# A two-layer hybrid decoder trunk on one core: residual rows, layer parameters and weight buffers placed differently

## The chip, the core and the metric

One core of a Trainium2 chip runs the whole program. TensorE (PE) does the matrix products, VectorE (DVE), ScalarE (ACT) and GpSimd (POOL) the elementwise work, and SyncE (SP) issues every DMA. The metric is the device time of one execution in microseconds, lower is better.

## What is computed

x is 1024 tokens by 1024 features in float32. Two layers (DEPTH = 2), each of them:

```
h = RMSNorm(x);  z = h @ w_in                       (1024 x 2560)
u = c_a * sigmoid(c_g);  u = silu(LayerNorm(dwconv31(u)))        (512 channels)
o = (softmax(q1 k1) - lam * softmax(q2 k2)) v      (4 heads, causal, rotary)
lam = exp(sum(lq1*lk1)) - exp(sum(lq2*lk2)) + lam_init
o = RMSNorm(o) * subln_g * (1 - lam_init)
x = x + RMSNorm(concat(u, o) @ w_out)
f = RMSNorm(x) @ w_up;  f = dwconv3(f);  f = gelu(f_g) * f_v
x = x + RMSNorm(f @ w_down)
```

The first four lines and w_out are called the mix here, the last two lines of the layer the FFN (up and down).

## The kernel before

Every float32 product runs as three passes (hi by hi, lo by hi, hi by lo). A weight block is therefore split: ACT copies the raw block to its rounded part (`whw`, `whq`, `wo`, `wp`; L460 and L1280), then DVE or POOL subtracts to get the rest (`wlw`, `wlq` at L466; L1281). A 512-wide product of one 128x128 block is one matmul; `hA` and `hB` hold the normalised rows of tokens 0 to 511 and 512 to 1023, transposed, in both parts.

A layer's mix (from L415) is ordered by a planner, `Flow` (L103): generators book time on four clocks (PE, DVE, ACT, POOL), wait for named events (`fl.set`), and take slots of rings (`Ring`) that stand for the tile buffers; a table of PE work (`TOKS`), one of conv taps (`TAPS`) and one of heads (`SEQ`) are its input. What the planner emits is the order of each engine. At the mix's end `wout` (L1059) multiplies by w_out, half of the columns and half of the tokens at a time (`dh`, `b`). `wout_half` (L1115) keeps the first half of the columns of a token tile, and for the second half of the tokens it also takes a buffer of the ring `e` and loads the residual rows x[4 + tt] into it (`xe`). `wout_post` (L1143) does the rest of a tile: the gain (L1154), the square sum on ACT (L1157), the reciprocal root (L350 on DVE, L352 on POOL), residual add (two operations, L1167 and L1168), store, square sum (L1173), root, and the next norm's rows `xn` (L1180). Tiles 0 to 3 take their `xn` from the ring `e` as well.

The FFN's up products run over a written sequence `seq` (L1583), with tasks hung beside its slots; rows of tiles 4 to 7 are transposed in it at L1331, and the products read `px`, `py`, `pz` banks that ACT and DVE empty (L1436 and after). Weight operands go through a ring `wo` of 7 tiles in the pool `fw_`, made by `parts` (L1277).

The down products are seven runs over 11 chunks each, in the order 1, 2, 5, 3, 6, 7, 4 (`run`, L1612), each with four token-tile banks `pd`; a chunk's operands are prepared three chunks ahead (L1280, L1281). During run 7 and run 4 one step of each generator `post_steps(tt)` (L1641) is taken per chunk: it finishes token tiles 0 to 3 (square L1648, gain L1649, root, residual add L1655 and L1656, store L1657, and for layer 0 the next layer's norm L1661 and L1665, transposes L1672, parts L1673 and L1675). Its residual rows come by `load_x` into the ring `xr`, which has two tiles. `end7` (L1714) folds run 7's bank of a tile into `vv`; run 4 then writes the same banks. After run 4, `postnorm` and `prenorm` (L380 to L402, L360 to L370) finish tiles 4 to 7; the next layer's mix begins with the products `pg` and `pa` (L496).

`params(l)` (L270) loads and works out a layer's small tensors; it is called at the start of each mix. PE, DVE, ACT and POOL keep the written order inside these blocks (`manual_schedule`); between the blocks a list scheduler places instructions. An engine executes in order, so an instruction that waits holds what stands behind it on its engine.

## Time and profile before

| | before |
|---|---|
| median of 3 runs | 2342.78 us (2337.95 to 2342.99) |
| profiled execution: time, span | 2336.54 us, 2334.4 us |
| granted TensorE clock, mean | 0.974 |
| PE busy | 2205.1 us, 94% |
| DVE / ACT / POOL busy | 1863.9 / 1126.9 / 829.9 us |

PE is busy for 94% of the span, so about 129 us of it are left in which PE does nothing. The stages of layer 0, by the last or first instruction of a kind: mix to 497.8 us, FFN up to about 945, down to 1176.3; layer 1's mix from 1185.7 to 1663.6, its FFN to the end. In the rows below a wait is the idle time of an engine before an instruction, with the instruction on another engine that ended it.

### The profile page before, as it was taken

How to read it: one execution, taken by the hardware profiler on the slowest of the kernel's cores; microseconds unless marked ns; L12 is line 12 of the kernel's file. 1: busy time of each engine (PE TensorE's matmuls, PEld its weight loads, DVE VectorE, ACT ScalarE, POOL GpSimd, SP SyncE). 2: the span in 40 equal slices, each digit the busy share in tenths (PEclk: the TensorE clock that was granted, in tenths of full speed). 3: DMA queues.
4: the chain of work that ended last, by engine and by line, in shares of the span. 5: the costliest groups of instructions: out<-in, count | busy, mean ns of one | idle time of the engine just before them, and what ended most of it. 6: DMA issues, size and time to landing. Idle time of an engine off the chain costs nothing. (4 is left out here: it accounts for less than half of the span.)

```text
span 2334.4 us, 31508 instructions
## 1 busy us (share of the span) xinstructions
PE 2205.1 (94%) x10568; PEld 1841.9 (79%) x10568; DVE 1863.9 (80%) x3287; ACT 1126.9 (48%) x2458; POOL 829.9 (36%) x894
## 2 busy tenths in 40 slices
PE   6999997989999999999879999979899999999998
PEld 5898895878877878788668988958788778787886
DVE  5988989657888888777669899896578888887777
ACT  4445456545444444544434454565454544445443
POOL 3324312235444544202433143122454555442024
PEclk9999997999999999999989999979999999999999
DMA  4313323544333334933333133235433333348343
GB/s 151 82 51 91 86 68 118 196 173 136 117 121 131 107 134 141 325 102 95 117 102 87 45 91 87 72 116 193 168 134 122 120 124 121 119 145 305 104 144 118
DMA packets 140129, 295.39 MB, mean 127 GB/s; under 512 B 16832, under 2 KB 33984, under 8 KB 139456
## 3 DMA queue, kind: packets, MB, share of 16 engines
q1 hardware_dynamic: 139968, 293.39, 39.3%
q8 instruction: 83, 1.36, 0.2%
q14 instruction: 78, 0.64, 0.1%
HBM read 198.44 MB, written 78.12 MB: 118 GB/s over the span
## 5 line engine op out<-in xcount | busy, mean ns | idle before, releaser
L1634 PE MATMUL pd<-wp,wo 128*128 128x512 f32 x1776 | 410.6, 393 | 10.8 <-DVE vv L1715 8.0
L1634 PEld LDWEIGHTS pd<-wp,wo 128*128 128x128 f32 x1776 | 334.7, 189 | 83.4 <-issue 7.4
L1583 PE MATMUL py<-t,wo 128*128 128x512 f32 x1584 | 377.4, 391 | 4.7 <-DVE cg L1451 4.7
L1583 PEld LDWEIGHTS py<-t,wo 128*128 128x128 f32 x1584 | 296.7, 188 | 73.5 <-ACT wo L1280 8.0
L1281 POOL TENSOR_TENSOR wo<-ws,wo 128x512 fp32r<-128x512 f32 x176 | 252.4, 1446 | 282.7 <-ACT wo L1280 250.9
L1583 PE MATMUL px<-hA,wo 128*128 128x512 f32 x1056 | 261.7, 400 | 14.9 <-ACT ea L1436 14.9
L1583 PEld LDWEIGHTS px<-hA,wo 128*128 128x128 f32 x1056 | 200.6, 191 | 64.0 <-ACT ea L1436 15.4
L1281 POOL TENSOR_TENSOR wo<-raw,wo 128x512 fp32r<-128x512 f32 x132 | 179.3, 1362 | 154.1 <-ACT wo L1280 149.4
L1281 POOL TENSOR_TENSOR wo<-fa,wo 128x512 fp32r<-128x512 f32 x66 | 101.6, 1555 | 322.7 <-ACT wo L1280 300.3
L1280 ACT ACTIVATE wo<-ws 128x512 fp32r<-128x512 f32 x176 | 108.4, 626 | 135.4 <-PE py L1583 49.6
L1469 DVE SCALAR_TENSOR_TENSOR acc<-cg,fw,acc 128x512 f32<-128x512 f32 x176 | 132.6, 753 | 41.7 <-ACT acc L1457 38.1
L594 DVE SCALAR_TENSOR_TENSOR scr<-u,cw,scr 128x256 f32<-128x256 f32 (+2 forms) x288 | 155.7, 558 | 2.0 <-ACT scr L588 1.8
L849 ACT ACTIVATE e<-S,mxv 128x512 f32<-128x512 f32 (+2 forms) x192 | 110.2, 581 | 66.5 <-DVE mxv L844 40.7
L854 POOL TENSOR_TENSOR sm<-sm 128x1 f32<-128x1 f32 x64 | 25.4, 398 | 328.7 <-ACT e L849 325.9
L1457 ACT ACTIVATE acc<-cg,fb,fw 128x512 f32<-128x512 f32 x88 | 68.2, 775 | 148.1 <-DVE cg L1451 148.1
L496 PE MATMUL pq<-whq,hA 128*128 128x384 f32 x512 | 134.8, 344 | 3.6 <-ACT whq L460 3.6
L496 PE MATMUL pq<-whq,hB 128*128 128x384 f32 x512 | 134.2, 343 | 0.0
L1583 PE MATMUL pz<-b,wo 128*128 128x512 f32 x528 | 131.0, 396 | 2.0 <-DVE cv L1451 2.0
L1583 PE MATMUL pz<-t,wo 128*128 128x512 f32 x528 | 130.5, 396 | 0.0
L1583 PEld LDWEIGHTS pz<-b,wo 128*128 128x128 f32 x528 | 98.3, 188 | 28.2 <-issue 5.1
L840 DVE TENSOR_REDUCE mxv<-S 128x1 f32<-128x512 f32 (+2 forms) x192 | 100.4, 547 | 22.9 <-PE S L824 18.2
L1583 PEld LDWEIGHTS pz<-t,wo 128*128 128x128 f32 x528 | 99.0, 188 | 23.6
(279 smaller groups left out, 5012.7 us busy)
## 6 DMA issues: line engine op xcount, KB each, us to landing
raw<-in_wupd SPq DMA_DIRECT2D x104, 512.0 KB, 3.6
fa<-f SPq DMA_DIRECT2D x154, 256.0 KB, 2.7
f<-fs SPq DMA_DIRECT2D x88, 256.0 KB, 3.1
raw<-in_wmix SPq DMA_DIRECT2D x80, 256.0 KB, 3.0
f<-gg SPq DMA_DIRECT2D x66, 256.0 KB, 2.0
raw<-in_wmix SPq DMA_DIRECT2D x64, 192.0 KB, 2.4
qs<-sth SPq DMA_DIRECT2D x64, 128.0 KB, 2.4
os<-onT SPq DMA_DIRECT2D x16, 512.0 KB, 3.0
```

What stands on the lines that cost most here:

```text
L496: mm = pe.matmul(dst, a, b, start=first and k + j == 0, stop=final and k == n - 1 and j == 2)
L594: ve.scalar_tensor_tensor(dst, src, wk, dst, op0=ALU.mult, op1=ALU.add)
L840: ve.tensor_reduce(mv_[:, j:j + 1], S, axis=AX.X, op=ALU.max, negate=True)
L849: se.activation(e[:, c0:c0 + w], S, AF.Exp, bias=mv_[:, 0:1], accum_out=sm[:, j:j + 1])
L854: po.tensor_tensor(sm[:, 0:1], sm[:, 0:1], sm[:, 1:2], op=ALU.add)
L1280: se.activation(w[:, 0], raw, AF.Copy)
L1281: eng.tensor_tensor(w[:, 1], raw, f32(w[:, 0]), op=ALU.subtract)
L1457: se.activation(acc[n, v, hf], C[n][v][:, 2 + hf * HB:2 + hf * HB + HB], AF.Identity, bias=fb[:, mt:mt + 1], scale=fw[:, mt, 2:3])
L1469: ve.scalar_tensor_tensor(dst, c[:, j + hf * HB:j + hf * HB + HB], fw[:, mt, j:j + 1], a, op0=ALU.mult, op1=ALU.add)
L1583: pe.matmul(ps, x, y, start=first and k + j == 0, stop=k == 3 and j == 2, skip_group_check=not first)
L1634: pe.matmul(ps[tt], x, y, start=first and k + n == 0, stop=k == K2 - 1 and n == 2, skip_group_check=not first)
```

## The change

Four edits. (1) `params` is a generator: DMAs first, then the operations, with two buffers per tensor; layer 1's run inside the mix of layer 0 (`next_params`, booked at 200 and 220 us of the planner's clock). (2) The `w` weights of the mix take their two tiles from a pool that lives for the whole program (`w4`, 4 tiles), and 4 of the 7 `wo` tiles of the FFN are the same four. (3) The residual rows of tiles 4 to 7 are loaded only once the four `xn` of tiles 0 to 3 have their buffers (`rows`). (4) The residual rows of `post_steps` go to two dead weight tiles, are loaded ahead of run 7 and refilled after a tile's store; the norm's `xr` tile is taken only then, one more step lies between the store and the square, and `end7` does its four additions first and the four `first_half` (gain and square) after them. No operation of the computation is left out or added.

```diff
@@ -268,37 +268,34 @@
         ve.memset(negh, -0.5)
         def params(l):
-            p = {}
+
             li = 0.8 - 0.6 * math.exp(-0.3 * l)
             def ptile(key, shape):
-                return par.tile(shape, F32, tag=key, name=f"{key}{l}", bufs=1)
-
-            cw = ptile("cw", [P, 4, CK])
+                return par.tile(shape, F32, tag=key, name=f"{key}{l}", bufs=2)
+
+            cw, cv, sg = ptile("cw", [P, 4, CK]), ptile("cv", [P, 3, 4]), ptile("sg", [P, 1])
             sy.dma_start(cw, ap["cw"][l])
+            sy.dma_start(cv, ap["cvec"][l])
+            sy.dma_start(sg, ap["subg"][l])
+            lv = par.tile([P, 4, HD], F32, tag="lv", name="lv", bufs=1)
+            sy.dma_start(lv, ap["lamv"][l:l + 1].broadcast_to([P, 4, HD]))
+            cws, hv, ls, nl = ptile("cws", [P, 4, (CK + 1) // 2]), ptile("hv", [P, 2, 4]), ptile("ls", [P, 2]), ptile("nl", [P, 1])
+            pars[l] = dict(cw=cw, cws=cws, cv=cv, hv=hv, sg=sg, nl=nl)
+            yield
...
             se.activation(ls, ls, AF.Exp)
-            nl = ptile("nl", [P, 1])
             ve.tensor_tensor(nl, ls[:, 1:2], ls[:, 0:1], op=ALU.subtract)
             ve.tensor_scalar(nl, nl, -li, None, op0=ALU.add)
-            p.update(cw=cw, cws=cws, cv=cv, hv=hv, sg=sg, nl=nl)
-            return p
+
+        pars = {}
         x1 = [[dr.tile([P, D], F32, tag=f"x1_{l}_{t}", name=f"x1_{l}_{t}") for t in range(8)] for l in range(DEPTH)]
         x2 = [[dr.tile([P, D], F32, tag=f"x2_{l}_{t}", name=f"x2_{l}_{t}") for t in range(8)] for l in range(DEPTH)]
@@ -424,7 +421,10 @@
                 if l == 0:
                     for t in range(8):
                         late[t] = prenorm(ptr, x0[t] if t < 3 else first_x(t), g_pre, hh[t // 4], t % 4)
-                p = params(l)
+                if l == 0:
+                    for _ in params(0):
+                        pass
+                p = pars[l]
                 wm = ap["wmix"][l]
                 bst = mx.tile([P, 480], F32, tag="bst", name="bst")[:, 0:192].rearrange("p (a b c) -> p a b c", a=8, b=4)
@@ -445,8 +445,11 @@
                     wi = yield from R[tag].get()
                     size, bufs = (768, 4) if tag == "q" else (1024, 2)
-                    hi = mw.tile([P, size], F32R, tag=f"wh{tag}", name=f"wh{tag}", bufs=bufs)
-                    lo = mw.tile([P, size], F32R, tag=f"wl{tag}", name=f"wl{tag}", bufs=bufs)
+                    if tag == "w":
+                        hi, lo = (rw.tile([P, 1024], F32R, tag="w4", name=f"w{part}w", bufs=4) for part in "hl")
+                    else:
+                        hi = mw.tile([P, size], F32R, tag=f"wh{tag}", name=f"wh{tag}", bufs=bufs)
+                        lo = mw.tile([P, size], F32R, tag=f"wl{tag}", name=f"wl{tag}", bufs=bufs)
                     W[key] = hi, lo, wi
                     step = n if n <= HB else n // 2
                     for j in range(n // step):
@@ -1054,7 +1057,7 @@
                     fl.set("oh", h, b)
                     yield fl.now
-                m0s, xe = {}, {}
+                m0s, xe, rows = {}, {}, []
                 def wout(dh, b):
@@ -1134,6 +1137,8 @@
                     fl.set("m0", b, tt)
                     yield t
                     if b == 1:
+                        if ("rows",) not in fl.seen:
+                            yield ("rows",)
                         i = yield from R["e"].get()
                         x = me.tile([P, D], F32, tag="e", name="xe", bufs=E_BUFS)
                         sy.dma_start(x, xres[4 + tt])
@@ -1211,6 +1216,9 @@
                     yield ("hA2",)
                     i = yield from R["e"].get()
                     xn = me.tile([P, D], F32, tag="e", name="xn", bufs=E_BUFS)
+                    rows.append(tt)
+                    if len(rows) == 4:
+                        fl.set("rows")
                     ss = xs.tile([P, 1], F32, tag="ss", name="ss", bufs=3)
                     se.activation(xn, y, AF.Square, accum_out=ss)
                     t = fl.op("act", ac(D) + 0.1)
@@ -1259,6 +1267,16 @@
                 for b in range(2):
                     fl.spawn(conv_ln(b))
                     fl.spawn(load_o(b))
+                def next_params():
+                    g = params(l + 1)
+                    yield 200.0
+                    next(g)
+                    yield 220.0
+                    next(g, None)
+                    fl.op("dve", 1.6)
+
+                if l + 1 < DEPTH:
+                    fl.spawn(next_params())
                 with tc.manual_schedule(engines={mybir.EngineType.PE, mybir.EngineType.DVE,
                                                  mybir.EngineType.Activation, mybir.EngineType.Pool}):
                     fl.run()
@@ -1276,10 +1294,18 @@
                 def parts(raw, eng, pool_=None, tag="wo", bufs=WO_BUFS):
-                    w = (pool_ or fw_).tile([P, 2, HB], F32R, tag=tag, name=tag, bufs=bufs)
+                    if pool_:
+                        w = pool_.tile([P, 2, HB], F32R, tag=tag, name=tag, bufs=bufs)
+                    else:
+                        w = ((rw.tile([P, 1024], F32R, tag="w4", name="wo", bufs=4) if turn[0] % WO_BUFS < 4 else
+                              fw_.tile([P, 1024], F32R, tag=tag, name=tag, bufs=WO_BUFS - 4))
+                             .rearrange("p (a b) -> p a b", a=2))
+                        turn[0] += 1
                     se.activation(w[:, 0], raw, AF.Copy)
                     eng.tensor_tensor(w[:, 1], raw, f32(w[:, 0]), op=ALU.subtract)
                     return w[:, 0], w[:, 1]
+
+                turn = [0]
                 def small(name):
                     return fw_.tile([P, HB], F32, tag="sr", name=name, bufs=4)
@@ -1644,7 +1670,7 @@
                         m0, s2 = m0s[tt]
                         ps1 = u2[tt]
                         y = xs.tile([P, YW], F32, tag="y", name="y", bufs=2)[:, 0:D]
-                        xr = load_x(x1[l][tt])
+                        xr = rows[tt % 2]
                         se.activation(y[:, 0:HB], ps1, AF.Square, accum_out=s2[:, 1:2])
                         ve.tensor_tensor(y[:, HB:D], ps1, g_pf[:, HB:D], op=ALU.mult)
                         yield 1
@@ -1655,8 +1681,12 @@
                         ve.scalar_tensor_tensor(y[:, 0:HB], m0, r, xr[:, 0:HB], op0=ALU.mult, op1=ALU.add)
                         ve.scalar_tensor_tensor(y[:, HB:D], y[:, HB:D], r, xr[:, HB:D], op0=ALU.mult, op1=ALU.add)
                         sy.dma_start(out[tt * P:(tt + 1) * P, :] if last else x2[l][tt], y)
+                        yield 1
+                        if tt < 2:
+                            sy.dma_start(rows[tt % 2], x1[l][tt + 2])
                         if last:
                             return
+                        xr = xs.tile([P, D], F32, tag="xr", name="xn", bufs=XR)
                         ss = xs.tile([P, 1], F32, tag="ss", name="ss", bufs=3)
                         se.activation(xr, y, AF.Square, accum_out=ss)
                         yield 1
@@ -1713,7 +1743,9 @@
                     def end7(tt):
                         ve.tensor_tensor(vv[tt], pa[tt], vv[tt], op=ALU.add)
-                        m0s[tt] = first_half(vv[tt], g_pf[:, HB:D], "m0d")
+                        if tt == 3:
+                            for t in range(4):
+                                m0s[t] = first_half(vv[t], g_pf[:, HB:D], "m0d")
                     def end4(tt):
                         t = 4 + tt
@@ -1737,6 +1769,9 @@
                     else:
                         g_pre = gvec(l + 1, 0)
                         nhA = alloc_h("hA")
+                    rows = [inB[1][:, i:i + 2].rearrange("p a b -> p (a b)") for i in (3, 5)]
+                    for tt in range(2):
+                        sy.dma_start(rows[tt], x1[l][tt])
                     bg = [post_steps(tt) for tt in range(4)]
                     run(7, pa, False, DTAIL, end7)
```

DVE at the border from the mix to the FFN (layer 0; layer 1 has the same). `pw` is a bank of the last w_out products, `xe` the residual rows, `xn` the next norm's rows. Before:

```order
L1167 SCALAR_TENSOR_TENSOR xe_5513<-m0_5469,rs_5651,xe_5513 128x512
L1168 SCALAR_TENSOR_TENSOR xe_5513<-xn_5634,rs_5651,xe_5513 128x512
L350 TENSOR_SCALAR ss_5656<-ss_5656 128x1
L350 TENSOR_SCALAR ss_5664<-ss_5664 128x1
L1180 SCALAR_TENSOR_TENSOR xn_5611<-xe_5350,rs_5662,gb0_2_5249 128x1024
L350 TENSOR_SCALAR ss_5669<-ss_5669 128x1
L1180 SCALAR_TENSOR_TENSOR xn_5620<-xe_5425,rs_5667,gb0_2_5249 128x1024
L1180 SCALAR_TENSOR_TENSOR xn_5634<-xe_5513,rs_5673,gb0_2_5249 128x1024
L1154 TENSOR_TENSOR xn_5679<-pw_5515,gb0_1_4233 128x512
L1162 TENSOR_TENSOR ss_5682<-s2_5520 128x1
L350 TENSOR_SCALAR ss_5682<-ss_5682 128x1
L1167 SCALAR_TENSOR_TENSOR xe_5677<-m0_5519,rs_5685,xe_5677 128x512
```

After:

```order
L1172 SCALAR_TENSOR_TENSOR xe_5535<-m0_5491,rs_5677,xe_5535 128x512
L1173 SCALAR_TENSOR_TENSOR xe_5535<-xn_5658,rs_5677,xe_5535 128x512
L347 TENSOR_SCALAR ss_5688<-ss_5688 128x1
L1172 SCALAR_TENSOR_TENSOR xe_5570<-m0_5541,rs_5686,xe_5570 128x512
L1173 SCALAR_TENSOR_TENSOR xe_5570<-xn_5668,rs_5686,xe_5570 128x512
L347 TENSOR_SCALAR ss_5696<-ss_5696 128x1
L1185 SCALAR_TENSOR_TENSOR xn_5635<-xe_5389,rs_5694,gb0_2_5271 128x1024
L347 TENSOR_SCALAR ss_5704<-ss_5704 128x1
L1185 SCALAR_TENSOR_TENSOR xn_5644<-xe_5447,rs_5702,gb0_2_5271 128x1024
L347 TENSOR_SCALAR ss_5710<-ss_5710 128x1
L1185 SCALAR_TENSOR_TENSOR xn_5658<-xe_5535,rs_5708,gb0_2_5271 128x1024
L1185 SCALAR_TENSOR_TENSOR xn_5668<-xe_5570,rs_5714,gb0_2_5271 128x1024
```

The fourth tile's gain (L1154 on `xn_5679`) stood behind three of the 1024-wide operations L1180; now all four tiles' residual adds (L1172, L1173) stand ahead of the four wide ones (L1185).

DVE at the end of run 7 in layer 0: `y` are the rows of tile 2, `vv` and `m0d` belong to end7. Before:

```order
L1675 TENSOR_TENSOR hA_0_10717<-pt_10979,hA_0_10717 128x4x128
L1665 SCALAR_TENSOR_TENSOR xr_10891<-y_10890,rs_10986,gb1_0_10715 128x1024
L1655 SCALAR_TENSOR_TENSOR y_10954<-m0d_9995,rs_10991,xr_10955 128x512
L1656 SCALAR_TENSOR_TENSOR y_10954<-y_10954,rs_10991,xr_10955 128x512
L1715 TENSOR_TENSOR vv_9482<-pd_10476,vv_9482 128x512
L380 TENSOR_TENSOR m0d_11039<-vv_9482,gb0_3_9426 128x512
L1715 TENSOR_TENSOR vv_9483<-pd_10477,vv_9483 128x512
L380 TENSOR_TENSOR m0d_11044<-vv_9483,gb0_3_9426 128x512
L1715 TENSOR_TENSOR vv_9484<-pd_10478,vv_9484 128x512
L380 TENSOR_TENSOR m0d_11049<-vv_9484,gb0_3_9426 128x512
L1715 TENSOR_TENSOR vv_9485<-pd_10479,vv_9485 128x512
L380 TENSOR_TENSOR m0d_11054<-vv_9485,gb0_3_9426 128x512
```

After:

```order
L1681 SCALAR_TENSOR_TENSOR y_10973<-m0d_10017,rs_11003,wbB_9483 128x512
L1682 SCALAR_TENSOR_TENSOR y_10973<-y_10973,rs_11003,wbB_9483 128x512
L1745 TENSOR_TENSOR vv_9504<-pd_10498,vv_9504 128x512
L1745 TENSOR_TENSOR vv_9505<-pd_10499,vv_9505 128x512
L1745 TENSOR_TENSOR vv_9506<-pd_10500,vv_9506 128x512
L1745 TENSOR_TENSOR vv_9507<-pd_10501,vv_9507 128x512
L377 TENSOR_TENSOR m0d_11053<-vv_9504,gb0_3_9448 128x512
L377 TENSOR_TENSOR m0d_11057<-vv_9505,gb0_3_9448 128x512
L377 TENSOR_TENSOR m0d_11061<-vv_9506,gb0_3_9448 128x512
L377 TENSOR_TENSOR m0d_11065<-vv_9507,gb0_3_9448 128x512
L1305 TENSOR_TENSOR wp_11074<-wb_9488,wp_11074 128x512
```

The wide norm operation of the tile before (L1665) stood ahead of the residual add and of `vv`; it now stands behind end7 (L1695), and the four `vv` follow one another.

ACT at the border from the FFN of layer 0 to the mix of layer 1: `y`, `xr` belong to the norms of tiles 4 to 7, `whw` to the first two weight tiles of the mix. Before:

```order
L360 ACTIVATE xr_11263,ss_11273<-y_11260 128x1024
L392 ACTIVATE y_11303,s2_11045<-s1_9492 128x512
L392 ACTIVATE y_11346,s2_11050<-s1_9493 128x512
L360 ACTIVATE xr_11306,ss_11316<-y_11303 128x1024
L296 ACT_TABLE_LOAD
L296 ACTIVATE ls1_11448<-ls1_11448 128x2
L392 ACTIVATE y_11389,s2_11055<-s1_9494 128x512
L460 ACTIVATE whw_11462<-raw_11464 128x512
L460 ACTIVATE whw_11462<-raw_11466 128x512
L460 ACTIVATE whw_11468<-raw_11470 128x512
L460 ACTIVATE whw_11468<-raw_11472 128x512
```

After:

```order
L463 ACTIVATE whw_11462<-raw_11464 128x512
L463 ACTIVATE whw_11462<-raw_11466 128x512
L1304 ACTIVATE wp_11254<-wb_9495 128x512
L389 ACTIVATE y_11282,s2_11054<-s1_9513 128x512
L357 ACTIVATE xr_11285,ss_11295<-y_11282 128x1024
L389 ACTIVATE y_11325,s2_11058<-s1_9514 128x512
L463 ACTIVATE whw_11468<-raw_11470 128x512
L463 ACTIVATE whw_11468<-raw_11472 128x512
L389 ACTIVATE y_11368,s2_11062<-s1_9515 128x512
L357 ACTIVATE xr_11328,ss_11338<-y_11325 128x1024
```

The four `whw` copies stood behind the last of the norms' squares and behind the table load and Exp of `params`; two of them now stand ahead of the first square (L389), two behind the second, and table load and Exp are gone from here (the load stands ahead of the first softmax Exp of layer 1's mix).

## Rows read from the trace of the kernel before

**Rows 1.** The longest waits of PE over the span: who waited, for which releaser, us in total, times, longest.

```profile
PE px L1583 <- ACT ea L1436: 14.9, 2, 7.4
...
PE pt L367 <- DVE ss L350: 13.4, 1, 13.4
...
PE o L924 <- ACT o L948: 10.4, 6, 2.5
...
PE pg L496 <- ACT whw L460: 9.4, 1, 9.4
...
PE pd L1634 <- DVE vv L1715: 8.0, 4, 7.1
```

**Rows 2.** PE's timeline at the border from mix to FFN, layer 0 and (last row) layer 1: start us, us, operation, count, idle before.

```profile
492.11 0.39 PE L496 MATMUL pw<-wlw,cat 128*128 128x512 f32 x1
...
497.79 5.75 PE L1583 MATMUL px<-hA,wo 128*128 128x512 f32 x24
...
504.05 1.07 PE L1331 MATMUL pt<-ident,xn 128*128 128x128 f32 x8 [0.51 <-DVE ss L350]
...
512.55 11.18 PE L1583 MATMUL px<-hA,wo 128*128 128x512 f32 x36 [7.44 <-ACT ea L1436]
...
1678.36 10.34 PE L1583 MATMUL px<-hA,wo 128*128 128x512 f32 x36 [7.44 <-ACT ea L1436]
```

**Rows 3.** DVE's timeline there, layer 0.

```profile
496.62 0.69 DVE L1154 TENSOR_TENSOR xn<-pw,gb 128x512 f32<-128x512 f32 x1 [0.41 <-PE pw L496]
...
505.59 1.28 DVE L1180 SCALAR_TENSOR_TENSOR xn<-xe,rs,gb 128x1024 f32<-128x1024 f32 x1 [0.44 <-POOL rs L352]
...
506.80 0.68 DVE L1154 TENSOR_TENSOR xn<-pw,gb 128x512 f32<-128x512 f32 x1
...
509.36 0.75 DVE L1167 SCALAR_TENSOR_TENSOR xe<-m,rs,xe 128x512 f32<-128x512 f32 x1 [0.72 <-POOL rs L352]
```

**Rows 4.** ACT's timeline there.

```profile
511.93 0.58 ACT L1436 ACTIVATE ea<-px 128x512 f32<-128x512 f32 x1
```

**Rows 5.** POOL's timeline there.

```profile
484.95 7.53 POOL L1281 TENSOR_TENSOR wo<-raw,wo 128x512 fp32r<-128x512 f32 x6 [0.63 <-ACT wo L1280]
...
496.35 0.54 POOL L352 TENSOR_TENSOR rs<-ss,negh 128x1 f32<-128x1 f32 x1 [3.86 <-DVE ss L350]
```

**Rows 6.** PE's timeline around the end of run 7, layer 0.

```profile
1124.92 5.74 PE L1634 MATMUL pd<-wp,wo 128*128 128x512 f32 x24
...
1137.71 5.37 PE L1634 MATMUL pd<-wp,wo 128*128 128x512 f32 x12 [7.05 <-DVE vv L1715]
...
1143.27 3.00 PE L1634 MATMUL pd<-wp,wo 128*128 128x512 f32 x12
...
1151.82 0.66 PE L1672 MATMUL pt<-ident,xr 128*128 128x128 f32 x4 [2.22 <-DVE hA L1675]
```

**Rows 7.** DVE's timeline around the end of run 7, layer 0.

```profile
1126.32 0.75 DVE L1655 SCALAR_TENSOR_TENSOR y<-m0d,rs,xr 128x512 f32<-128x512 f32 x1 [1.86 <-DMA xr<-x]
...
1130.65 1.34 DVE L1281 TENSOR_TENSOR wp<-wb,wp 128x512 fp32r<-128x512 f32 x1 [2.32 <-ACT wp L1280]
...
1133.46 2.18 DVE L1665 SCALAR_TENSOR_TENSOR xr<-y,rs,gb 128x1024 f32<-128x1024 f32 x1
...
1136.89 0.68 DVE L1715 TENSOR_TENSOR vv<-pd,vv 128x512 f32<-128x512 f32 x1
```

**Rows 8.** ACT's timeline in run 7, layer 0.

```profile
1127.82 1.06 ACT L1661 ACTIVATE xr<-y 128x1024 f32<-128x1024 f32 x1 [6.27 <-DVE y L1656]
```

**Rows 9.** PE's timeline at the border from layer 0's FFN to layer 1's mix.

```profile
1157.00 19.31 PE L1634 MATMUL pd<-wp,wo 128*128 128x512 f32 x84
...
1185.72 0.79 PE L496 MATMUL pg<-hA,whw 128*128 128x512 f32 x1 [9.41 <-ACT whw L460]
...
1207.21 0.69 PE L496 MATMUL pq<-whq,hA 128*128 128x384 f32 x2 [3.64 <-ACT whq L460]
```

**Rows 10.** ACT's timeline there.

```profile
1181.89 1.28 ACT L296 ACT_TABLE_LOAD   x1
...
1184.43 0.63 ACT L392 ACTIVATE y<-s 128x512 f32<-128x512 f32 x1 [1.04 <-DVE nl L299]
...
1185.05 2.17 ACT L460 ACTIVATE whw<-raw 128x512 fp32r<-128x512 f32 x4
```

**Rows 11.** POOL's timeline there.

```profile
1185.81 4.98 POOL L466 TENSOR_TENSOR wlw<-raw,whw 128x512 fp32r<-128x512 f32 x4 [1.41 <-ACT whw L460]
```

**Rows 12.** Busy time by stretch: from:to, length, then busy us and count of PE, PEld, DVE, ACT and POOL, the granted clock, the DMA share, GB/s.

```profile
1185.50:1191.00 5.50, 4.65 (x11) 3.41 (x12) 0.00 (x0) 1.73 (x4) 4.98 (x4) 0.54 0.30 88
...
1207.00:1212.00 5.00, 4.05 (x11) 2.76 (x11) 5.00 (x6) 2.97 (x7) 3.83 (x3) 0.56 0.50 156
...
200.00:400.00 200.00, 182.64 (x1030) 160.93 (x1029) 178.21 (x422) 106.88 (x315) 54.23 (x90) 0.91 0.29 84
```

**Rows 13.** The group of the second residual add of tiles 4 to 7 in layer 0: shortest, median, longest duration in ns, first and last start.

```profile
L402 DVE SCALAR_TENSOR_TENSOR y<-y,rs,xr x4: 744/1119/1503, 1173.4 to 1207.6; 128x512 f32<-128x512 f32 x4
```

**Rows 14.** ACT's timeline at the first softmax Exp of layer 1's mix.

```profile
1246.67 0.37 ACT L849 ACTIVATE e<-S,mxv 128x128 f32<-128x128 f32 x1 [3.06 <-DVE mxv L840]
```

**Rows 15.** SP's timeline in the first mix: three raw weight loads, and the load of x tile 6.

```profile
25.09 2.80 SPq L456 DMA_DIRECT2D raw<-in_wmix  x3
27.98 0.38 SPq L242 DMA_DIRECT2D xr<-in_x  x1
```

More of the change, by code (lines that the diff above doesn't have):

```diff
@@ L270, in params @@
         def params(l):
-            p = {}
             li = 0.8 - 0.6 * math.exp(-0.3 * l)
             def ptile(key, shape):
-                return par.tile(shape, F32, tag=key, name=f"{key}{l}", bufs=1)
-            cw = ptile("cw", [P, 4, CK])
+                return par.tile(shape, F32, tag=key, name=f"{key}{l}", bufs=2)
+            cw, cv, sg = ptile("cw", [P, 4, CK]), ptile("cv", [P, 3, 4]), ptile("sg", [P, 1])
             sy.dma_start(cw, ap["cw"][l])
+            sy.dma_start(cv, ap["cvec"][l])
[5 more added lines that the diff above has]
+            yield
             ve.tensor_scalar(cw, cw, 0.5, None, op0=ALU.mult)
-            cws = ptile("cws", [P, 4, (CK + 1) // 2])
             ve.tensor_copy(cws[:, :, 0], cw[:, :, 0])
@@ L283, in params @@
             ve.tensor_tensor(cws[:, :, 1:], cw2[:, :, 0], cw2[:, :, 1], op=ALU.add)
-            cv = ptile("cv", [P, 3, 4])
-            sy.dma_start(cv, ap["cvec"][l])
-            hv = ptile("hv", [P, 2, 4])
             ve.tensor_scalar(hv, cv[:, 1:3, :], 0.5, None, op0=ALU.mult)
-            sg = ptile("sg", [P, 1])
-            sy.dma_start(sg, ap["subg"][l])
             ve.tensor_scalar(sg, sg, (1.0 - li) * math.sqrt(P), None, op0=ALU.mult)
-            lv = xs.tile([P, 4, HD], F32, tag="m0", name="lv", bufs=4)
-            sy.dma_start(lv, ap["lamv"][l:l + 1].broadcast_to([P, 4, HD]))
-            ls = ptile("ls", [P, 2])
             ve.tensor_tensor(lv[:, 0:2, :], lv[:, 0:2, :], lv[:, 2:4, :], op=ALU.mult)
```

## Prediction

> **What bounds the kernel now.** I read the page's first part, the table of PE's waits, then the timelines of PE and of its releasers at the largest. PE is busy 94% of the span, so matmuls set the time, and since the change leaves their number alone, only PE's idle time and its clock can move. The waits [rows 1] show where: 14.9 us in two equal pieces at the borders from mix to FFN, 9.4 us at the border from layer 0's FFN to layer 1's mix, 8.0 us for `vv` in the down stage (one piece of 7.1), 13.4 us at the start, and many small ones in the attention. The first three are what the edits touch. After such waits the clock is at its lower level for a while: 0.54 in the 5.5 us behind the 9.4 us wait [rows 12].
>
> **Border mix to FFN (edits 2 and 3, twice).** PE ends its first 24 `px` products at 503.5, does eight transposes at 504.05 and then stands 7.44 us until 512.55 [rows 2]. It waits for the copy `ea` on ACT, which starts at 511.93 [rows 4], directly behind the square of the fourth token tile. That tile is late on DVE: its gain L1154 runs at 506.80 behind the wide operations, 10.2 us after the third tile's at 496.62, and its residual add only at 509.36 [rows 3]. Nothing in the data asks for that, because its bank is full when the w_out products end at 497.8. It is the place in the order, which came from the ring `e`. After the change the four adds stand together ahead of the wide operations.
>
> The new bound is POOL. Today its last six `wo` subtractions run from 484.95, 7.53 us or 1.255 each, and its first root follows at 496.35 [rows 5]. Now four of the seven `wo` tiles are the mix's `w` tiles, and the third and fourth must wait for the last readers of the last `whw` and `wlw`, products that end about 492.3 [rows 2]. ACT's copies wait in their order there, with `wo` five to seven and the squares of the w_out tiles queued behind; on POOL five subtractions wait, with all the roots behind them. So POOL has 492.3 + 0.6 for a copy + 5 x 1.255 = 499.2, and the first root is out at 499.8. Four pairs of adds at 2 x 0.75 [rows 3] end at 505.8; the first wide operation (1.28) gives 507.1, the transposes (1.07) with a signal 508.3, and the square and `ea` are done by then. PE goes on at 508.3 instead of 512.55, so 4.25 us per border, 8.5 for the two, which stand at the same 7.44 us [rows 2]. What stays idle is near 4 us. A wait of 3.64 us in this kernel [rows 9] was followed by a clock of 0.56 [rows 12], so I count nothing for the clock: 36 products now take 11.18 and 10.34 us where 24 in 5.75 make it 8.63 [rows 2], and that loss of 2.55 and 1.71 may stay. Bounds: 0, if the `w` tiles come free only with the last w_out product at 497.8 (then POOL ends 5.5 later and eats the gain); 18.6 in all, if POOL does not delay the roots (the first is out at 496.9 today, so 2.9 more at each border) and the clock's 4.3 come back too. I take -8.5.
>
> **End of run 7 in layer 0 (edit 4).** PE ends run 7 at 1130.66 and waits 7.05 us for `vv`, whose addition begins at 1136.89 [rows 6, 7]. DVE lost the time in three pieces: 1.86 us idle before L1655 for the residual rows of tile 2 (their load waits for one of two `xr` tiles), 2.32 us idle before a `wp` part, because ACT stood in a square that itself waited 6.27 us for DVE's `y` [rows 7, 8], and 2.18 us of L1665 run ahead of `vv`. The loads ahead of run 7 take the first; the step between store and square moves the square behind the next copies, which takes the second; the order above takes the third. 1136.89 less 6.36 is 1130.5, about when PE ends, so about 0.9 us (one addition and the signal) stays of 7.05: -6.1. The clock after it costs 5.37 - 3.00 = 2.4 us today [rows 6], and a gap of 0.9 should not cost it. But the same work comes back in run 4: four gains of 0.69 (the duration of the same shape in [rows 3]) and the two wide operations now run beside its first products, where transposes already wait 2.22 us for DVE's `hA` [rows 6]. I put +2.0 for that. Sum -6.5; bounds 0 (all of the moved work ends on a transpose wait) and -10.7 (7.05 + 2.4 + 2.2 less the 0.9). The extra loads are as many as before; they only come earlier and no queue shown here is full. In layer 1 the same wait is the small rest of the 8.0 us [rows 1].
>
> **Border FFN to mix (edits 1 and 2).** PE ends run 4 at 1176.3 (1157.00 + 19.31) and waits 9.41 us for the first `whw` [rows 9]. ACT makes it at 1185.05, behind a table load, the Exp of lambda and a square that waited 1.04 us for DVE's `nl` [rows 10]; POOL's rest follows at 1185.81 [rows 11]. With `w4` the copies stand ahead of the norms' squares, and the first wait only for old readers. The first `wlw` is then ready within one 1.25 us piece (4.98 over four) of the last down product [rows 11]. The full price is 9.41 plus the clock: 4.65 us of products at 0.54 [rows 12] lose 2.1. Against it: up to 1.25 for the first piece, and a delay of tile 5's root behind four pieces on POOL, which its transposes, some 12 us on, can bear. The pieces also no longer run while DVE is idle (0.00 busy at 1185.5 to 1191, [rows 12]) but beside its norms. The second residual add of tiles 4 to 7 takes 744 ns at the shortest and 1503 at the longest, the long ones being those beside POOL's `wlq` [rows 13]; three such operations meet the pieces, so 3 x 0.76 at most, and I take 0.8. Sum -9.5; bounds -11.5 and -5 (the later waits for `whq`, 3.64 us [rows 9], growing by the amount gained up front).
>
> The Trainium skill (SBUF — State Buffer, section "SBUF: two separate sides") says that DVE operations with two SBUF inputs and GpSimd share one port pair as an exclusive lock, where the loser waits out the whole instruction. The doubled add in [rows 13] agrees. By that rule each of the three operations could wait a full 1.25 us piece, 3.8 instead of my 0.8, and the border would give -6.5.
>
> The table load (1.28 us, [rows 10]) does not vanish; it moves ahead of the first softmax Exp, where ACT is idle 3.06 us for the row maximum [rows 14]. Cover holds: 0; without it +1.3.
>
> **Start and the first mix.** SP's loads come in another order: x tile 6 is no longer issued behind the second and third of three raw loads (27.98, [rows 15]) and comes some 2 us earlier, while four small loads and layer 1's parameters are put before raw weights. Bounds -3 and +1; I take -1. In the first mix layer 1's nine small DVE operations (1.6 us by the planner's own booking in the diff) enter a stretch where DVE is busy 178 of 200 us and PE idle 17.4 [rows 12], and the planner, told of them, orders it anew from there. I take 0, with 5 either way.
>
> Sum: -8.5 - 6.5 - 9.5 - 1.0 = -25.5. Against the profiled execution's 2336.54 that is 2311.0; that execution lies 6.2 below the median of 2342.78, and the next median should lie as much above its profile, so 2317.
>
> **Rivals.**
> 1. The shared ring turns into the wait at both kinds of border: `wo` and `wlw` wait for the last products, POOL's pieces stand ahead of all roots. For: five subtractions of 1.255 stand right ahead of the roots in a chain with 1.5 us pairs behind. Against: the readers end 5 us before the last product. Then the first term is 0 and the third -5: -12.5, about 2330.
> 2. Gains are given back a little later, as the next thing is late anyway: run 4's transposes take -6.5 to -2, and the waits for `whq` take -9.5 to -5. For: PE waits there today (2.22 and 3.64). Against: those waits hang on steps that move forward with PE. -16.5: 2326.
> 3. More than forecast: the clock stays up at the mix borders too (4.3), run 7 gives 10.7, the mix 5 more. -25.5 - 4.3 - 4.2 - 5 = -39, 2304 in full; with half of the extra 2310.
> 4. Slower: the new order of the first mix. It is one re-planning from about 220 us on in a stretch with no slack on DVE (89%). Its price today is 17.4 us idle and a clock of 0.91, which on 182.6 us of products is at most 16 more [rows 12]. It decides from 30 us on (the 25.5 of the borders and 4.7 that can be measured), so if nearly both double; both doubled, 33, give 2342.8 - 25.5 + 33 = 2350. For: `o` waits of 2.5 us already pile up in this chain [rows 1]. Against: what is put in is 1.6 us.
>
> **How the numbers follow.** Forecast 0.45, rival 1 0.12, rival 2 0.17, rival 3 0.15, rival 4 0.05, and 0.06 for two rivals at once that leave no change. What this kernel can tell from no change is 0.2%, 4.7 us. The range is from 2303 (rival 3 nearly in full) to 2333 (rival 1 with its second bound). Faster 0.88, same 0.07, slower 0.05.
>
> **What would show it.** Right: PE's two waits for `ea` at 3 to 4.5 us each, the `vv` wait near 1, `pg` starting within 2 us of the last `pd`, and the waits in the first mix within 5 us of 17.4. Wrong: roots on POOL at the mix border later than 500 us, a new wait of PE for `wlw`, longer waits for `hA` in run 4 or for `whq` and `wlq` after the border. The prediction falls if the first mix grows by over 10 us, or if two of the three borders keep their waits.

## The result, and the profile after

The changed kernel took 2315.11 us (median of 4 runs, 2312.5 to 2316.61), the kernel before 2342.42 (median of 4). The ratio is 0.9886, 95% interval 0.9869 to 0.9903. The profiled execution took 2314.21 us, its span is 2312.4, its clock 0.979.

PE is busy a little less than before, and most of the gain is idle time. From the page's first part:

```profile
PE 2202.4 (95%) x10568; PEld 1838.5 (80%) x10568; DVE 1879.3 (81%) x3287; ACT 1126.7 (49%) x2458; POOL 832.6 (36%) x894
```

The large waits of PE over the span (us in total, times, longest); the three of [rows 1] that the edits touch are gone or smaller:

```profile
PE pt L1357 <- DVE ss L347: 7.8, 2, 3.9
...
PE pq L499 <- ACT whq L463: 3.9, 1, 3.9
...
PE pt L1702 <- DVE xn L1695: 3.9, 2, 3.4
...
PE pd L1660 <- DVE vv L1745: 2.0, 1, 2.0
...
PE pg L499 <- POOL wlw L469: 0.7, 1, 0.7
```

**Border mix to FFN.** PE's timeline in layer 0, to be read against [rows 2]: one wait of 3.88 us ahead of the transposes, and none behind them.

```profile
497.71 5.60 PE L1609 MATMUL px<-hA,wo 128*128 128x512 f32 x24
...
507.19 1.94 PE L1357 MATMUL pt<-ident,xn 128*128 128x128 f32 x8 [3.88 <-DVE ss L347]
...
508.79 9.31 PE L1609 MATMUL px<-hA,wo 128*128 128x512 f32 x36
```

POOL's timeline there (against [rows 5]): five subtractions that wait for the shared tiles, and then at once two roots.

```profile
492.95 6.31 POOL L1305 TENSOR_TENSOR wo<-raw,wo 128x512 fp32r<-128x512 f32 x5 [7.30 <-ACT wo L1304]
...
499.22 1.04 POOL L349 TENSOR_TENSOR rs<-ss,negh 128x1 f32<-128x1 f32 x2
```

DVE's (against [rows 3]): the first residual add directly behind the first root, and the first wide operation behind the four pairs.

```profile
499.79 0.75 DVE L1172 SCALAR_TENSOR_TENSOR xe<-m,rs,xe 128x512 f32<-128x512 f32 x1 [0.98 <-POOL rs L349]
...
505.77 1.28 DVE L1185 SCALAR_TENSOR_TENSOR xn<-xe,rs,gb 128x1024 f32<-128x1024 f32 x1
```

**End of run 7 in layer 0.** PE (against [rows 6]): 2.03 us of wait for `vv` in place of 7.05, and 3.42 in place of 2.22 at a transpose.

```profile
1120.42 5.71 PE L1660 MATMUL pd<-wp,wo 128*128 128x512 f32 x24
...
1128.59 5.79 PE L1660 MATMUL pd<-wp,wo 128*128 128x512 f32 x24 [2.03 <-DVE vv L1745]
...
1137.80 0.63 PE L1702 MATMUL pt<-ident,xn 128*128 128x128 f32 x4 [3.42 <-DVE xn L1695]
```

DVE (against [rows 7]): the residual add L1681 takes 1.77 us, and the four `vv` follow as one group. POOL's row shows the `wo` piece that runs beside L1681.

```profile
1125.42 1.77 DVE L1681 SCALAR_TENSOR_TENSOR y<-m0d,rs,wbB 128x512 f32<-128x512 f32 x1 [0.37 <-POOL rs L349]
...
1127.77 2.47 DVE L1745 TENSOR_TENSOR vv<-pd,vv 128x512 f32<-128x512 f32 x4
```

```profile
1125.36 1.28 POOL L1305 TENSOR_TENSOR wo<-fa,wo 128x512 fp32r<-128x512 f32 x1
```

**Border FFN to mix.** PE (against [rows 9]): no wait ahead of `pg`, 0.71 us for the first `wlw`, and the later wait for `whq` as long as ever.

```profile
1166.11 0.40 PE L499 MATMUL pg<-hA,whw 128*128 128x512 f32 x1
...
1167.22 0.50 PE L499 MATMUL pg<-hA,wlw 128*128 128x512 f32 x1 [0.71 <-POOL wlw L469]
...
1188.86 1.01 PE L499 MATMUL pq<-whq,hA 128*128 128x384 f32 x2 [3.92 <-ACT whq L463]
```

POOL's and DVE's timelines there (against [rows 11]): the four `wlw` pieces take 6.45 us where they took 4.98, and a wide norm operation 2.28.

```profile
1165.90 6.45 POOL L469 TENSOR_TENSOR wlw<-raw,whw 128x512 fp32r<-128x512 f32 x4
```

```profile
1165.96 2.28 DVE L359 SCALAR_TENSOR_TENSOR xr<-y,rs,gb 128x1024 f32<-128x1024 f32 x1
```

The stretch behind the border (columns as in [rows 12]): the clock is 1.00 where it was 0.54.

```profile
1166.00:1172.00 6.00, 5.29 (x24) 4.05 (x23) 5.20 (x5) 1.54 (x4) 6.00 (x4) 1.00 0.28 80
```

Cut at the same instructions of PE (first `px` of a layer's FFN, second transposes behind it, first `pd`, first `pg`, the end), the two traces give this account in us:

| stage | before | after | difference |
|---|---|---|---|
| start and first mix | 497.79 | 497.71 | -0.1 |
| border mix to FFN, layer 0 | 25.78 | 20.22 | -5.6 |
| FFN up, layer 0 | 421.63 | 421.08 | -0.6 |
| down, run 7, border to the first `pg` | 240.52 | 227.10 | -13.4 |
| mix of layer 1 | 477.89 | 478.70 | +0.8 |
| border mix to FFN, layer 1 | 24.93 | 20.13 | -4.8 |
| FFN up, layer 1 | 421.36 | 421.34 | 0.0 |
| down, layer 1 | 224.50 | 226.12 | +1.6 |

The sum is -22.0, the difference of the spans. The medians differ by 27.3: the profiled execution of before lies 5.9 below this median of four (6.2 below the median of three that the prediction used), that of the changed kernel 0.9.

### The profile page after: what moved, and what is told of

Same layout as the page of the kernel before. It is cut to its first block, busy times and chain, and to the rows that moved or that the text cites. A ratio compares the mean times of both kernels' runs of the same rounds, so it can differ in the third digit from the quotient of the medians.

```text
span 2312.4 us, 31516 instructions
## 1 busy us (share of the span) xinstructions
PE 2202.4 (95%) x10568; PEld 1838.5 (80%) x10568; DVE 1879.3 (81%) x3287; ACT 1126.7 (49%) x2458; POOL 832.6 (36%) x894
## 5 line engine op out<-in xcount | busy, mean ns | idle before, releaser
L1609 PE MATMUL px<-hA,wo 128*128 128x512 f32 x1056 | 255.3, 394 | 0.0
L857 POOL TENSOR_TENSOR sm<-sm 128x1 f32<-128x1 f32 x64 | 25.5, 398 | 316.9 <-ACT e L852 301.6
L843 DVE TENSOR_REDUCE mxv<-S 128x1 f32<-128x512 f32 (+2 forms) x192 | 100.5, 549 | 24.1 <-PE S L827 18.2
```

Of the source, the lines that this page charges most:

```text
L843: ve.tensor_reduce(mv_[:, j:j + 1], S, axis=AX.X, op=ALU.max, negate=True)
L857: po.tensor_tensor(sm[:, 0:1], sm[:, 0:1], sm[:, 1:2], op=ALU.add)
L1609: pe.matmul(ps, x, y, start=first and k + j == 0, stop=k == 3 and j == 2, skip_group_check=not first)
```

## Experiments

All ratios are to the kernel before, timed on the same chip. The changed kernel once more, beside three of the others, gave 2313.50 us and 0.9891 (0.9876 to 0.9906).

> The changed kernel once more, on the chip of the next three, to compare with: 0.9886 of the kernel before, within 0.002.

**Edit 3 taken back (e1).**

```diff
-                        if ("rows",) not in fl.seen:
-                            yield ("rows",)
...
-                    rows.append(tt)
-                    if len(rows) == 4:
-                        fl.set("rows")
```

> The changed kernel without edit 3: the residual rows of tiles 4 to 7 take their buffers as before, the rest stays. My theory: the gain at the mix borders comes from this edit alone, so PE's wait for ea comes back (7 to 10 us per border, since POOL's late subtractions now hit the old order), and the time is 10 to 16 us above the changed kernel, 2325 to 2331 us. Rival: the gain there came from the new buffers of the weights; then the border keeps its wait of 3.9 us and the time stays within 3 us of 2315.

2327.07 us, 0.9951 (0.9935 to 0.9967), 12 us above the changed kernel. PE's wait for `ea` is back behind the transposes (7.39 us in layer 0, 6.50 in layer 1), on top of 3.03 us ahead of them, so the border is longer than in the kernel before (27.3 and 27.7 us by the cuts of the table). Edit 3 makes the gain at this border; the shared tiles without it make the border worse. PE's timeline in layer 0:

```profile
513.72 10.38 PE L1604 MATMUL px<-hA,wo 128*128 128x512 f32 x36 [7.39 <-ACT ea L1457]
```

**Edit 2 taken back (e2).**

```diff
-                    if tag == "w":
-                        hi, lo = (rw.tile([P, 1024], F32R, tag="w4", name=f"w{part}w", bufs=4) for part in "hl")
-                    else:
-                        hi = mw.tile([P, size], F32R, tag=f"wh{tag}", name=f"wh{tag}", bufs=bufs)
...
+                    w = (pool_ or fw_).tile([P, 2, HB], F32R, tag=tag, name=tag, bufs=bufs)
```

> The changed kernel without edit 2: the mix's w weights and the seven operand tiles are in the stages' own pools again. My theory: the FFN to mix border loses what it gained (about 9.4 us of wait and 1.9 of clock, +11), while at the two mix borders POOL no longer waits, its first root is out near 497 instead of 499.8, and each border gains 2 to 3 us (-5): some 2321 us, 3 to 8 above the changed kernel. Rival: that border was held by the parameters on ACT, not by the weights' space; then it stays short and the time falls to 2308 to 2312.

2320.25 us, 0.9921 (0.9905 to 0.9937), 5 us above the changed kernel. As expected, the 9.1 us wait for `whw` is back, although layer 1's parameters still run early, at 271.50 us. At the mix borders PE waits 2.45 us ahead of the transposes in place of 3.88, so 1.4 less, where I had put 2 to 3: with POOL free, DVE's fourth gain and four pairs set the start, the first pair at 498.67. By the cuts of the table the two borders are 1.1 us shorter (19.07 and 19.10), but that alone would show nothing: in six executions of the changed kernel's order there (it, its second run, e3, e4, e7 and e8) the same cuts gave 18.6 to 21.5, as the 36 products behind the wait took 8.5 to 10.6 us. DVE's timeline, then PE's at the two borders:

```profile
498.67 0.74 DVE L1169 SCALAR_TENSOR_TENSOR xe<-m,rs,xe 128x512 f32<-128x512 f32 x1
```

```profile
506.07 1.94 PE L1348 MATMUL pt<-ident,xn 128*128 128x128 f32 x8 [2.45 <-DVE ss L347]
...
507.66 9.44 PE L1600 MATMUL px<-hA,wo 128*128 128x512 f32 x36
...
1171.91 0.80 PE L496 MATMUL pg<-hA,whw 128*128 128x512 f32 x1 [9.13 <-ACT whw L460]
```

Something I had not looked for showed here too: layer 1's down stage takes 222.70 us in this kernel and 226.12 in the changed one, with no wait to account for it. It is taken up below.

**Edit 4 taken back (e3), and its two pieces alone (e7, e8).**

```diff
e3
-                        xr = rows[tt % 2]
+                        xr = load_x(x1[l][tt])
...
-                        yield 1
-                        if tt < 2:
-                            sy.dma_start(rows[tt % 2], x1[l][tt + 2])
...
-                        if tt == 3:
-                            for t in range(4):
-                                m0s[t] = first_half(vv[t], g_pf[:, HB:D], "m0d")
+                        m0s[tt] = first_half(vv[tt], g_pf[:, HB:D], "m0d")
e7 (the loads stay; the step and the grouped end7 go)
-                        yield 1
...
-                        if tt == 3:
-                            for t in range(4):
-                                m0s[t] = first_half(vv[t], g_pf[:, HB:D], "m0d")
+                        m0s[tt] = first_half(vv[tt], g_pf[:, HB:D], "m0d")
e8 (the step and the grouped end7 stay; the loads go)
-                        xr = rows[tt % 2]
+                        xr = load_x(x1[l][tt])
...
```

> The changed kernel without edit 4: the residual rows of tiles 0 to 3 by way of the two xr tiles, no step between store and square, end7 as before. My theory: the 7 us wait for vv and the low clock behind it come back, 4.5 to 6.5 us, 2320 to 2322 us, and only that place changes. Rival: what edit 4 gave at vv it gave back in run 4 and at the border, so that the time is within 2 us of the changed kernel.

> Of edit 4 only the early loads into dead weight tiles; the square follows the store at once and end7 is as before. My theory: the loads take away the 1.9 us that DVE waited for a row, no more, so the wait for vv stays at 4 to 6 us, and the time is 3 to 5 us above the changed kernel. Rival: the loads were what held it all, as ACT's square and the rest hung on them; then the wait is 2.5 us or less and the time within 1.5 us.

> Of edit 4 only the step between store and square and the grouped end7; the residual rows come by way of the two xr tiles again. My theory: with the loads alone the wait for vv was 6.1 us, without edit 4 6.8 and with all of it 2.0, so step and order carry some 4 us of it and the loads add the rest only behind them: the wait is 2.5 to 4.5 us here, the time 1 to 3 us above the changed kernel. Rival: each piece is useless without the others, and the wait stays at 6 us or more, the time 6 above.

e3: 2321.53 us, 0.9927 (0.9909 to 0.9944); e7: 2322.86, 0.9924 (0.9909 to 0.9939); e8: 2319.97, 0.9915 (0.9894 to 0.9936). By the ratios to the kernel before, edit 4 as a whole is worth 8 to 10 us, and each piece alone nothing that can be told from e3. The wait for `vv` is 6.81 us without the edit, 6.06 with the loads alone, 7.79 with step and order alone, 2.03 with all of it. My expectation for e7 fell on the time (3 to 5 us above the changed kernel; 9.4 above its second run came), the one for e8 on the wait (2.5 to 4.5 us), and e8's rival held for the wait. That only this place would change (e3) did not hold either: layer 1's down stage takes 227.4 us in e3 and e7, where the changed kernel and e8 take 226.1 and 226.2. The step and the grouped `end7` were not tried apart. PE's rows, e3, e7 and e8 in turn:

```profile
1136.66 5.44 PE L1660 MATMUL pd<-wp,wo 128*128 128x512 f32 x12 [6.81 <-DVE vv L1741]
```

```profile
1135.89 5.43 PE L1660 MATMUL pd<-wp,wo 128*128 128x512 f32 x12 [6.06 <-DVE vv L1744]
```

```profile
1133.70 7.93 PE L1660 MATMUL pd<-wp,wo 128*128 128x512 f32 x24 [7.79 <-DVE vv L1742]
```

DVE's timelines say why. With the loads alone (e7) DVE waits 2.33 us for ACT's `wp`, since ACT still stands ahead of a square (L1690) that waits 5.26 us for DVE's `y`. ACT's row, then DVE's:

```profile
1125.97 1.06 ACT L1690 ACTIVATE xn<-y 128x1024 f32<-128x1024 f32 x1 [5.26 <-DVE y L1682]
```

```profile
1128.81 1.37 DVE L1305 TENSOR_TENSOR wp<-wb,wp 128x512 fp32r<-128x512 f32 x1 [2.33 <-ACT wp L1304]
```

With the step and the grouped `end7` alone (e8) the rows come through two tiles that are now held a step longer, and DVE waits 3.34 and 5.08 us for them:

```profile
1121.98 0.75 DVE L1681 SCALAR_TENSOR_TENSOR y<-m0d,rs,xr 128x512 f32<-128x512 f32 x1 [3.34 <-DMA xr<-x]
...
1131.53 0.75 DVE L1681 SCALAR_TENSOR_TENSOR y<-m0d,rs,xr 128x512 f32<-128x512 f32 x1 [5.08 <-DMA xr<-x]
```

Each piece only removes the wait that the other leaves last.

**Edit 1's move taken back (e4).**

```diff
-                if l == 0:
-                    for _ in params(0):
-                        pass
+                for _ in params(l):
+                    pass
...
-                if l + 1 < DEPTH:
-                    fl.spawn(next_params())
```

> The changed kernel without the move of layer 1's parameters: they are worked out at the start of layer 1's mix again (two buffers as in the changed kernel). My theory: with the weights in their own tiles the copies of whw no longer stand behind the table load, so the FFN to mix border gets at most 3 us longer, and the first mix returns to the old order, which cost the same: within 3 us of the changed kernel, 2313 to 2318. Rival: the parameters on ACT were the larger part of the 9.4 us wait; then the border waits 5 us or more again and the time is 2321 or above.

2312.04 us, 0.9889 (0.9873 to 0.9905): no difference to the changed kernel. PE's row at the border is the same, 0.71 us for `wlw`. But the run is not what I had meant. In the kernel before, the Exp of layer 1's parameters ran at 1183.18 us, behind the table load of [rows 10]; here it ran at 35.05, in the first mix, with no table load of its own. My guess, which no run shows, is that with two buffers per tensor nothing holds these operations back, and the list scheduler puts them there. So e4 says only that 35 us and 272 us, where the changed kernel has them, are equally good. What the border needed is shown by e2: with the parameters early and the weights without tiles of their own, 9.13 of the 9.41 us stay. Whether those tiles alone would do, with the table load and the Exp still at the border, no run shows. ACT's row of the Exp in the kernel before, then in e4, then PE's at the border:

```profile
1183.18 0.20 ACT L296 ACTIVATE ls<-ls 128x2 f32<-128x2 f32 x1
```

```profile
35.05 0.20 ACT L294 ACTIVATE ls<-ls 128x2 f32<-128x2 f32 x1 [3.38 <-DVE ls L293]
```

```profile
1165.26 0.50 PE L498 MATMUL pg<-hA,wlw 128*128 128x512 f32 x1 [0.71 <-POOL wlw L468]
```

**Other tiles of the ring shared (e5), and together with e4's edit (e6).**

```diff
-                        w = ((rw.tile([P, 1024], F32R, tag="w4", name="wo", bufs=4) if turn[0] % WO_BUFS < 4 else
+                        w = ((rw.tile([P, 1024], F32R, tag="w4", name="wo", bufs=4) if turn[0] % WO_BUFS >= 3 else
```

> The changed kernel with one comparison turned: of each seven operand tiles the first three come from the FFN's own pool and the last four are shared with the mix, instead of the first four. My theory (POOL's five subtractions behind the ring's wait hold the roots): only two of the seven wait for the last w_out products now, POOL is free by 496, PE's wait at each mix border falls from 3.9 to 2.4 us, the value without shared tiles; the first wlw is no longer waited for at the FFN to mix border (0.7); 3 to 5 us less than the changed kernel. Rival: the roots are set by DVE's order alone, and nothing changes by more than 1 us.

> The turned comparison and layer 1's parameters at the start of its mix together. My theory: the gains add up, since they lie at other places: 2 us of the first mix (it ended at 495.9 with the parameters late, at 497.7 with them inside) and the 3 to 5 us of the turned comparison, so 5 to 7 us less than the changed kernel. Rival: the parameters on ACT now hold the copies of whw, which would stand ready early, and the sum is less than the turned comparison alone.

e5: 2304.43 us, 0.9848 (0.9834 to 0.9863), about 10 us below the changed kernel; e6: 2305.87, 0.9846 (0.9829 to 0.9863). In e5 only two pieces wait, POOL ends them at 497.2 and is free when the first root's input comes (idle 0.79 for it), and PE waits 2.44 us ahead of the transposes. The first `wlw` is no longer waited for. POOL's timeline, then PE's at both borders:

```profile
494.65 2.54 POOL L1305 TENSOR_TENSOR wo<-raw,wo 128x512 fp32r<-128x512 f32 x2 [3.61 <-ACT wo L1304]
...
497.98 0.54 POOL L349 TENSOR_TENSOR rs<-ss,negh 128x1 f32<-128x1 f32 x1 [0.79 <-DVE ss L347]
```

```profile
507.61 1.06 PE L1357 MATMUL pt<-ident,xn 128*128 128x128 f32 x8 [2.44 <-DVE ss L347]
...
1165.78 0.39 PE L499 MATMUL pg<-hA,whw 128*128 128x512 f32 x1
...
1166.01 0.39 PE L499 MATMUL pg<-hA,wlw 128*128 128x512 f32 x1
```

The gain is more than the 3 to 5 us expected; the places named give 1.4 us twice and 0.7, and layer 1's mix is 5 us shorter (473.4 by the table's cuts, 473.4 in e6 as well). Of these, the waits of PE for POOL in that mix hold some: they were 2.2 us for `wlq` and 0.7 for `wlw` in the changed kernel, and are 0.4 in e5, 2.5 less. PE's waits from 1160 to 1660 us, the changed kernel and then e5:

```profile
PE pq L499 <- POOL wlq L469: 2.2, 5, 0.6
```

```profile
PE pq L499 <- POOL wlq L469: 0.4, 1, 0.4
```

By the traces the 5 us are all idle time of PE: it is idle for 29.9 us of this mix in the changed kernel and for 24.3 in e5, and busy for the same 449. Beside the 2.5 us these are small waits in the attention, the longest 1.6 us for a DMA to `kk1A`; what ties them to the order of the tiles no run singles out. The place of the operands, which the next part is about, is not it: e5 has 2784 products at unlike offsets and the changed kernel 2856. In e6 layer 1's parameters ran at 34.57 us, as in e4, so that its rival, parameters that hold the copies of `whw`, could not show. The 2 us that e6 was to add did not come: the end of the first mix lies at 498.8 in a second run of the changed kernel and at 495.4 in e8, with the same order there, so that my reading of e4's 495.9 was run-to-run difference.

**The offset of operands (e9, e10, e11).** The down stage's loss in the changed kernel has no wait in it. In a stretch where PE is busy throughout, the same 120 us hold fewer matmuls: 531 before, 521 in the changed kernel (columns as in [rows 12]).

```profile
960.00:1080.00 120.00, 120.00 (x531) 99.40 (x530) 91.69 (x140) 57.56 (x105) 7.17 (x5) 1.00 0.51 159
```

```profile
960.00:1080.00 120.00, 120.00 (x521) 97.66 (x520) 88.78 (x141) 54.02 (x99) 1.35 (x1) 1.00 0.46 141
```

I took the start-to-start times of the 512-wide products from the traces and sorted them by where the programs place their operands (four shared tiles in one pool, three in another). What separates them is whether the stationary and the moving operand have the same byte offset within 64; here the offsets are 0 or 32.

```
mean ns from one product's start to the next into the same bank (count)
            same offset     32 bytes apart
before  px  -               233.3 (964)
        py  228.8 (1486)    -
        pz  -               233.5 (960)
        pd  226.9 (1798)    -
after   px  227.0 (554)     233.2 (421)
        py  228.9 (628)     233.3 (858)
        pz  228.7 (544)     233.4 (416)
        pd  227.6 (804)     233.2 (1009)
```

The shared tiles have offset 32, like `hA`; the FFN's own had 0, like `wp`. So the edit speeded some `px` and `pz` and slowed more of `py` and `pd`: 2856 products at unlike offsets (the expectation below counts 2855), 2112 before. 744 more at 6.2 ns make 4.6 us, an estimate from these paces.

```diff
                 fw_ = pool(st, f"fw{l}", bufs=1, reuse_waits="tile")
+                fw_.tile([P, 8], F32, tag="pad", name="pad")
```

> The changed kernel with 32 unused bytes ahead of the FFN's pool, nothing else; all 512-wide products then have both operands at the same offset within 64 bytes. Matched products followed each other after 227.0 ns in the changed kernel's trace, the 2855 products whose two operands lay 32 bytes apart within 64 after 233.2 ns. Theory (the offset sets the pace): all come at 227 to 229, 2855 x 5.5 ns = 16 us less, of which the FFN's waits for VectorE give back up to a third: 10 to 16 us below the changed kernel. Rival (the pace hangs on which pool a tile is in, or on the distance of the operands): the mixed paces stay, and the time is within 2 us of it.

> The turned comparison (first three of seven operand tiles from the FFN's own pool) with the 32 bytes. If both act where I think, they add: 9 + 10 to 16 us, so 18 to 25 below the changed kernel, 2288 to 2296 us. Rival: the offset does nothing, 2304 us.

> The kernel before with the 32 bytes. It has 2112 products at unlike offsets (px and pz), so by the offset theory 2112 x 6 = 13 us less at most, 8 to 13 below the kernel before. The distance to the changed kernel with the 32 bytes is then 30 us rather than 27, since the change itself had put 743 more products at unlike offsets. Rival: no change within 2 us.

e9 (the changed kernel with the 32 bytes): 2299.98 us, 0.9832 (0.9813 to 0.9851), against 0.9891 some 14 us less. The changed kernel was not timed beside it, so the ratios to the kernel before are what can be compared. e11 (the kernel before with them): 2328.16, 0.9948 (0.9925 to 0.9972), 12 less. e10 (with e5's order): 2291.15, 0.9798 (0.9782 to 0.9815), the best of all and faster than both kernels. Nothing but 32 unused bytes differs between e9 and the changed kernel, the shared tiles stay where they were, and the stretch holds 531 matmuls again. The bytes move the other tiles of the pool as well, but PE alone gets faster: it is busy for 2181.8 us in e9 and for 2202.4 in the changed kernel, the other engines within 4 us of what they were. In e9 and e11 both operands lie at 32, and the mean paces are 226.8 to 227.3 ns, as for `pd` in the kernel before, where both lie at 0. So it is the two offsets agreeing that sets the pace, not the offset of one of them and not the pool. Part of the gain comes back as waits: PE's for `cg` in the up stage grew from 5.8 to 8.2 us.

```profile
PE 2181.8 (95%) x10568; PEld 1837.3 (80%) x10568; DVE 1883.1 (82%) x3287; ACT 1125.9 (49%) x2458; POOL 832.5 (36%) x894
```

```profile
960.00:1080.00 120.00, 120.00 (x531) 99.38 (x530) 87.83 (x141) 55.12 (x100) 4.34 (x3) 1.00 0.44 139
```

```profile
PE py L1610 <- DVE cg L1478: 8.2, 8, 1.3
```

What the change lost by this shows best in the down stages, where the kernel before had no product at unlike offsets and the changed kernel has 1032: by the cuts of the table the 32 bytes take 2.7 and 3.2 us off the two down stages of the changed kernel (to 224.39 and 222.90), and 0.3 off and 0.2 on in the kernel before (240.26 and 224.71). For the whole programs, 14 and 12 us, the difference is 2 us rather than 4.6, and the intervals are wider than that.

Not tried: other offsets than these, and the reason inside the chip. That it is 64 bytes that count is not shown either, as the operands that agree here agree within 256 bytes too.

## Why the prediction was right, and where not

The forecast was 2317 us for the median, 2311.0 for the profiled execution; 2315.1 and 2314.2 came. In the spans the change gave 22.0 us where 25.5 were forecast. That the median came within 2 us is luck: its distance to the profiled execution, put at 6.2 us, was 0.9, which covered the rest.

- **Border mix to FFN, -8.5 forecast.** The chain came as worked out: POOL done with the five subtractions at 499.26 (said 499.2), first pair at 499.79 (499.8), wide operation at 505.77 (505.8), PE on its way at 508.79 (508.3). The stage gained 5.6 and 4.8, since "I count nothing for the clock" was too careful: 36 products took 9.31 and 9.21 us instead of 11.18 and 10.34. How much of that comes is not fixed; in the six executions named under e2 they took 8.5 to 10.6. Rival 1 had the mechanism right that held the gain down; e5 took it away.
- **Run 7, -6.5.** PE's wait fell by 5.0 of the 6.1 forecast. The mis-sized term is the 0.9 us left: 2.03 came, as L1681 took 1.77 us for 0.75 while POOL worked on a `wo` piece. The +2.0 for work that returns measured 1.2 in one transpose wait (3.42 for 2.22). From run 7's last product to run 4's last the traces take 45.65 and 40.14 us, so 5.5 came of the 6.5. A step failed that the sum hid: "DVE lost the time in three pieces", each taken off by one part of the edit. e7 and e8 show that the times do not add up piece by piece: the wait for `vv` stays at 6.06 and 7.79 us with part of the edit and falls to 2.03 only with all of it.
- **Border FFN to mix, -9.5.** From run 4's end to the second transposes of the next mix it was 24.1 us and is 12.6, so -11.5: the whole wait and the clock. Waits for `whq` and `wlq` behind it came as before (6.1 for 5.8), not longer, against rival 2. The table load, now at 1222.78 us, is covered as forecast: ACT still waits 1.83 us for the row maximum behind it. I had put "edits 1 and 2" together; e2 shows that edit 1 without edit 2 gives next to nothing here (9.13 us of wait for 9.41), and whether edit 2 needs edit 1 stays open.
- **POOL beside DVE there, +0.8.** The four pieces took 1.5 us longer and one wide operation 1.0, more than I took. The Trainium skill (SBUF — State Buffer, "SBUF: two separate sides") says that a DVE operation with two SBUF inputs and a GpSimd operation that reads SBUF exclude each other for a whole instruction; the trace agrees, with an L1681 of 1.77 us beside a POOL piece of 1.28, where it takes 0.75 alone. At this border PE waited no longer for it: behind the 0.71 us for `wlw` it has no wait until `wlq`.
- **Start and first mix, -1.** -0.1, within what two runs of one kernel differ there.
- **The step that failed:** "since the change leaves their number alone, only PE's idle time and its clock can move." The pace of the single product moved, by the place of its operands. By the estimate above that cost the change 4.6 us over all; in the down stages alone, where it cost most, 5.9 us came back with the 32 bytes. It stood in no term and no rival. The two kinds of border, which gave some 2 us each more than forecast, made up for part of it.

## What to carry to other kernels

Where an operation waits for three things in a row, take the last one away only together with those that become last behind it, and try the parts singly before giving them credit. Before a run is read as "without X", look up in its trace where X ran: e4 had its parameters somewhere else than its edit meant. When buffers of two stages are shared, share those that the later stage needs last. And when a stage gets slower with no wait, count matmuls in a busy stretch before and after: buffers that move in memory can change their pace.

## What the runs showed of the hardware

At a granted clock of 1.00 a 512-wide product of this kernel (float32r operands, 128x128 by 128x512) follows the one before after 227 to 229 ns when its two operands have the same byte offset within 64, and after 233.2 to 233.5 ns when they lie 32 apart. 32 unused bytes in one pool gave 14 us of 2314, and 12 of 2340 in the kernel before.
